# Activations laid out chunk by chunk, first part and rest, tokens of one parity together

## The chip, the cores and the metric

The kernel runs on one core of one Trainium2 chip. The metric is the device time of one execution in microseconds, median over runs; less is better.

## The reference

A two-layer encoder on 256 tokens of 1024 channels, float32. Cut to what matters:

```python
for layer in range(DEPTH):                       # DEPTH = 2
    h = h + token_mixer(rmsnorm(h, norm1), ...)  # sub-layer 1
    h = h + conv_ffn(rmsnorm(h, norm2), ...)     # sub-layer 2
return rmsnorm(h, norm_f)

def token_mixer(xn, ...):
    u, q, k, v, g_pool, g_attn = split(xn @ w_in)     # 1024, 3 x 1536, 2 x 1024 columns
    pooled   = [centred_mean(u of group, window w) - u of group for w in (2, 4, 8, 16)]
    pool_out = (pooled @ w_pool per group) * pool_scale
    attn_out = dilated sliding-window attention, 3 groups of 4 heads of 128, combined
    return (sigmoid(g_pool) * (pool_out @ w_a) + sigmoid(g_attn) * (attn_out @ w_b)) @ w_o

def conv_ffn(xn, ...):
    a, g = split(xn @ w_up)                            # 2816 columns each
    a = depthwise convolution of width 3 along the tokens (a) + conv_b
    return (gelu(a) * g) @ w_down
```

## The kernel before

Every float32 product is made of three products in a reduced float32 format: a number is kept as a first part (a cast) and a rest (the number less the cast), for weights (`wh`, `wl`, lines L177 and L178, by ScalarE and VectorE) and for activations (names ending in `h` and `l`). A product is first x first, first x rest and rest x first, summed in PSUM.

Tokens are dealt by parity: token 2m + t sits in partition m of slot t wherever rows are tokens (`h`, `v`). Where channels are the partitions, an activation was kept as 256 tokens in their order, in tiles of shape `[P, 2, KD, S]` (part, chunk of 128 channels, token).

There are two forms of product.

*Channels out* (`proj`, L485 and L486; `chunk_mm`, L475 to L477). The weight chunk (128x128) is stationary and the activation moves. `proj` makes for each of eight chunks a pair: L485 has `wh` stationary and moves first part and rest together, `x2[:, :, k, :]`, 512 columns that lie in two runs of 256; L486 has `wl` stationary and moves the 256 columns of the first part. Both write one PSUM tile of 512, whose halves are added by `add_up` (L492 on ScalarE, L493 on VectorE) or by lines L951 to L963 for q and k. `proj` is called for u, q, k, the gates, `po @ w_a` and both halves of `w_up`.

*Tokens out* (`v_sum`, L567; `residual_mm`, L497 to L499). 128 tokens of one parity of the activation are stationary, `a[:, k, t::2]`, so every second word; 512 columns of weights move. Used for v, for the four first chunks of the MLP's a (the "entry"), for `w_o` and for `w_down`. For layer 0's v, L640 and L729 do the same from `xuh` and `xul`, which are kept as `[P, KD, 2, P]` (parity, then token of that parity).

The tiles in question: `x2` (the normalised input, written by `to_channels` L454 and L455, in layer 0 by `first_values` L716 and L717), `plh`/`pll` (pooled, L821 and L822), `po2` (pooling's output, L837 and L838), `at2` (attention's output, L920 and L921), `m2` (merged, L1006 and L1007) and `acth`/`actl` (the MLP's activation, L1100 and L1101). Pooling (L802 to L816) and convolution (L1074 to L1078) work along the tokens in order.

The order of work is the program's. A class `Weights` loads weights through SP's queue some pieces ahead and splits them three pieces ahead of use; two pools of four PSUM tiles (`acc`, `mmp`) hold the products. Between stages, after a residual product, the first products of the next stage on one parity are put between the transposes of the other (`fill`).

Of the kernel before, what the change touches and what calls it, by code (L numbers as in the profile page):

```python
# [16 lines left out]
P = 128  # L17
# [187 lines left out]
def encoder(ctx, tc, x, w_in, w_pool, pool_scale, w_a, w_b, w_o, norm1, norm2, w_up, conv_w,  # L205
# [225 lines left out]

    def to_channels(xh, xl, psum, g):

        tag = "acc" if psum is acc else "mm"

        def fin(t, r, xn):
            for n in range(4):
                cc = slice(n * 256, (n + 1) * 256)  # L440
                nc.vector.scalar_tensor_tensor(
                    out=xn[:, cc], in0=h[:, t, cc], scalar=r[:, 0:1], in1=g[:, cc],
                    op0=ALU.mult, op1=ALU.mult,
                )
            for n in range(2):
                pt = psum.tile([P, 4, P], F32, tag=tag, name="xt_ps")
                ks = slice(4 * n, 4 * n + 4)
                for k in range(4):
                    c0 = (4 * n + k) * P
                    nc.tensor.transpose(pt[:, k, :], xn[:, c0 : c0 + P], ident)  # L450
                oh = xh[:, ks, :].rearrange("p k (m t) -> p k t m", t=2)[:, :, t, :]
                ol = xl[:, ks, :].rearrange("p k (m t) -> p k t m", t=2)[:, :, t, :]
                last = [
                    nc.scalar.copy(out=oh, in_=pt),  # L454
                    nc.vector.tensor_sub(out=ol, in0=pt, in1=oh.bitcast(F32)),  # L455
                ]
# [15 lines left out]
    def chunk_mm(ps, wh, wl, xh, xl, nk):  # L472

        for k in range(nk):
            nc.tensor.matmul(ps, wh(k), xh[:, k, :], start=(k == 0), stop=False)  # L475
            nc.tensor.matmul(ps, wh(k), xl[:, k, :], start=False, stop=False)  # L476
            nc.tensor.matmul(ps, wl(k), xh[:, k, :], start=False, stop=(k == nk - 1))  # L477

    def proj(x2, nk=8):


        i, (wh, wl) = W.get()
        ps = mmp.tile([P, 2, S], F32, tag="mm", name="proj_ps")
        for k in range(nk):
            nc.tensor.matmul(ps, wh[:, k, :], x2[:, :, k, :], start=(k == 0), stop=False)  # L485
            nc.tensor.matmul(ps[:, 1], wl[:, k, :], x2[:, 0, k, :], start=False, stop=(k == nk - 1))  # L486
        W.free(i)
        return ps[:, 0], ps[:, 1]

    def add_up(out, sums):  # L490
# [10 lines left out]
    def residual_mm(parts, n, done, hold=4, fill=None):  # L501
# [59 lines left out]

    def v_sum(ps, xh, xl, t, n, piece):

        _, (wh, wl) = piece
        passes = [(xh, wh, 0), (xh, wl, 0), (xl, wh, 0), (xh, wh, 1), (xh, wl, 1), (xl, wh, 1)]
        for m, (a, w, j) in enumerate(passes):
            nc.tensor.matmul(  # L567
                ps, a[:, 2 * n + j, t::2], w[:, j, :], start=(n + m == 0), stop=(n == 3 and m == 5)
            )
# [127 lines left out]
    def first_values(rs, raw_x, fs, done, pe, keep_values):  # L697

        xuh, xul = raw_x
        xh, xl, x2 = channel_tiles()  # L700

# [35 lines left out]
    for l in range(DEPTH):  # L737
# [21 lines left out]
        if l == 0:  # L759
            with tc.manual_schedule():  # L760
                begun = begin_values_of_x()
            x2 = first_values(*begun, keep_values)
            xh, xl = x2[:, 0], x2[:, 1]
        else:
            for g in range(NG):
                held = begun[0] if g == 0 else [W.get() for _ in range(4)]
                for t in range(2):
                    if g + t == 0:
                        ps = begun[1]
                    else:  # L770
                        ps = v_tile()
                        for n in range(4):
                            v_sum(ps, xh, xl, t, n, held[n])
                    keep_values(t, g, ps)
# [9 lines left out]

        plh = big.tile([P, KD, S], F32R, tag="ybig", name="plh")
        pll = big.tile([P, KD, S], F32R, tag="xn", name="pll")
        pooled = {}
        for gi in range(3, -1, -1):
# [30 lines left out]
            )  # L819
            ph, pl = plh[:, 2 * gi : 2 * gi + 2, :], pll[:, 2 * gi : 2 * gi + 2, :]  # L820
# [3 lines left out]
        def pool_out(poh, pol):  # L824
            for j in range(2):
                i, (wh, wl) = W.get()
                for gg in range(2):
                    ph, pl = pooled[2 * j + gg]
                    for oc in range(2):
                        ps = mmp.tile([P, S], F32, tag="mm", name="pool_ps")  # L830
                        cc = slice(oc * P, (oc + 1) * P)
# [4 lines left out]
                        sc = hps[:, l, c : c + 1]  # L836
                        nc.scalar.activation(poh[:, c, :], ps, AF.Copy, scale=sc)  # L837
                        nc.vector.scalar_tensor_tensor(  # L838
                            out=pol[:, c, :], in0=ps, scalar=sc, in1=poh[:, c, :].bitcast(F32),
                            op0=ALU.mult, op1=ALU.subtract,  # L840
# [9 lines left out]
        kk = big.tile([P, NH - HPG, 2, P], F32, tag="k1", name="k")  # L850
        at2 = big.tile([P, 2, HPG, S], F32R, tag="at2", name="at2")
        ath, atl = at2[:, 0], at2[:, 1]
# [51 lines left out]
        def weigh(hh):  # L904
# [6 lines left out]
            for g in (1, 2):  # L911
                hd = (g - 1) * HPG + hh
                for t in range(2):
# [20 lines left out]
        for m, c in enumerate(PAIRS):  # L934
            if m == 1:
                po2 = big.tile([P, 2, KD, S], F32R, tag="m2", name="po2")
                poh, pol = po2[:, 0], po2[:, 1]
                pool_parts = pool_out(poh, pol)
            if m == 2:
# [45 lines left out]
        for c in range(KD):  # L985
# [3 lines left out]
            )  # L989
        m2 = big.tile([P, 2, KD, S], F32R, tag="m2", name="m2")  # L990
        mh, ml = m2[:, 0], m2[:, 1]
        for c4 in range(2):
            ths = [gate(4 * c4 + j) for j in range(4)]
            for j2 in range(2):
                i, (wh, wl) = W.get()
                for j in range(2):
# [8 lines left out]
                    nc.vector.tensor_add(out=m, in0=m, in1=pa[:, c, :])  # L1005
                    nc.scalar.copy(out=mh[:, c, :], in_=m)  # L1006
                    nc.vector.tensor_sub(out=ml[:, c, :], in0=m, in1=mh[:, c, :].bitcast(F32))  # L1007
                W.free(i)

        xh, xl, x2 = channel_tiles()  # L1010
        norm = Norm(to_channels(xh, xl, acc, g2))
        entry = []

        def begin_mlp():
# [3 lines left out]
            for n in range(3):  # L1018
                v_sum(ps, xh, xl, 0, n, held[n])
            entry.extend((held, ps))  # L1020
            return lambda: v_sum(ps, xh, xl, 0, 3, held[3])

        run(residual_mm(lambda k: (mh[:, k, :], ml[:, k, :]), KD, norm.add, fill=begin_mlp))


# [3 lines left out]
            [  # L1029
                big.tile([P, n, S], F32R, tag=f"{tag}{j}", name=f"act{tag}{j}")  # L1030
                for j, n in enumerate((HPG, NH - HPG))
# [23 lines left out]
        for n in range(4):  # L1055
            v_sum(ps, xh, xl, 1, n, held[n])
            if n == 1:
# [7 lines left out]
        def up(f):  # L1065
# [15 lines left out]
            )  # L1081
            g = sm.tile([P, S], F32, tag="p", bufs=3, name="g")
            add_up(g, sums)

# [14 lines left out]
            ah, al = (x[n >= HPG][:, n - HPG * (n >= HPG), :] for x in (acth, actl))  # L1099
# [7 lines left out]
        def begin_values():  # L1107

            ps, held = v_tile(), [W.get() for _ in range(4)]
            for n in range(3):  # L1110
                v_sum(ps, xh, xl, 0, n, held[n])
            begun.extend((held, ps))
            return lambda: v_sum(ps, xh, xl, 0, 3, held[3])

# [10 lines left out]
        if l + 1 < DEPTH:  # L1125
            xh, xl, x2 = channel_tiles()
            late["norm"] = Norm(to_channels(xh, xl, mmp, g1))
        else:
# [32 lines left out]
```

## Time and profile before

| | |
|---|---|
| median of 3 runs | 891.43 us (890.87 to 891.78) |
| profiled execution: own time, span | 890.68 us, 888.9 us |
| TensorE busy, matmuls | 881.2 us (99%), 4913 |
| VectorE busy | 671.2 us (76%) |
| ScalarE busy | 516.0 us (58%) |
| GpSimd busy | 13.7 us (2%) |
| DMA, mean | 185 GB/s, 164.47 MB |
| granted TensorE clock | 0.999 |

How to read it: busy is the time in which an engine had an instruction running. Matmuls are pipelined: the trace gives each a duration that overlaps the next one's, so the sum of durations is more than their time, and the interval from one start to the next tells what one costs. PE is the matmuls, PEld the loads of stationary operands, which overlap them; DVE is VectorE, ACT ScalarE, POOL GpSimd.

### The profile page before, as it was taken

Reading aid. Unit: us, or ns where it says so; the run is one execution under the profiler, and the core shown is the slowest. Engines: PE = TensorE matmul, PEld = TensorE weight load, DVE = VectorE, ACT = ScalarE, POOL = GpSimd, SP = SyncE. Lnnn points to the kernel's source line nnn. Section 1 sums busy time; section 2 is a strip of 40 time slices with the busy share of each in tenths; the row PEclk is TensorE's granted clock in tenths of the full one; section 3 lists DMA queues with packets and bytes.
Section 4 is the critical chain, followed back from the end, with each engine's and each line's share of the span. In section 5 each row is a group of like instructions: output and inputs, shape, how many; then the busy total and the mean of one; then the engine's idle time right before and its main releaser. Section 6 shows DMA issues by size and latency. Waiting matters only on the chain.

```text
span 888.9 us, 12895 instructions
## 1 busy us (share of the span) xinstructions
PE 881.2 (99%) x4913; PEld 764.5 (86%) x4913; DVE 671.2 (76%) x1135; ACT 516.0 (58%) x897; POOL 13.7 (2%) x40
## 2 busy tenths in 40 slices
PE   9999999999999999999999999999999999999997
PEld 7889889889888888888888898888898888888886
DVE  7988786767759978777855977766677698777784
ACT  7746454555647756666545564554555476666662
POOL 2000000000000000000000000000000000000000
PEclk9999999999999999999999999999999999999999
DMA  9669744455545465565636555443557346465531
GB/s 335 227 206 302 235 143 142 144 189 189 188 168 190 153 227 190 168 211 189 237 119 211 168 190 189 144 161 125 190 189 264 106 155 231 166 202 187 180 143 48
DMA packets 125791, 164.47 MB, mean 185 GB/s; under 512 B 2996, under 2 KB 106108, under 8 KB 125601
## 3 DMA queue, kind: packets, MB, share of 16 engines
q1 hardware_dynamic: 125712, 163.65, 55.1%
q8 instruction: 38, 0.62, 0.3%
q14 instruction: 25, 0.20, 0.1%
q10 hardware_dynamic: 16, 0.00, 0.0%
HBM read 162.57 MB, written 3.69 MB: 187 GB/s over the span
## 4 chain that ended last, share of the span: by engine, by line
PE 99%; ACT 0%; POOL 0%; DVE 0%; issue 0%; POOLq 0%; ACTq 0%
PE proj_ps L485 40%; PE proj_ps L486 20%; PE v_ps L567 6%; PE res_ps L497 6%; PE res_ps L499 6%; PE res_ps L498 6%; PE v_ps L729 2%; PE v_ps L640 1%; PE b_ps L477 1%; PE b_ps L475 1%; PE b_ps L476 1%; PE pt_ps L893 1%; PE o_ps L914 1%; PE s_ps L864 1%; PE s_ps L859 1%; PE o_ps L910 1%
## 5 line engine op out<-in xcount | busy, mean ns | idle before, releaser
L485 PE MATMUL proj_ps<-x,wh 128*128 128x512 f32 x1408 | 498.4, 398 | 0.0
L178 DVE TENSOR_TENSOR wl<-raw,wh 128x1024 fp32r<-128x1024 f32 x274 | 334.5, 1224 | 131.0 <-ACT wh L177 129.3
L177 ACT CAST wh<-raw 128x1024 fp32r<-128x1024 f32 x274 | 287.2, 1052 | 201.3 <-PE proj_ps L485 144.6
L486 PE MATMUL proj_ps<-x,wl 128*128 128x256 f32 x1408 | 394.3, 280 | 0.0
L485 PEld LDWEIGHTS proj_ps<-x,wh 128*128 128x128 f32 x1408 | 264.4, 188 | 63.3 <-issue 0.7
L486 PEld LDWEIGHTS proj_ps<-x,wl 128*128 128x128 f32 x1408 | 265.7, 189 | 1.0 <-issue 0.2
L497 PE MATMUL res_ps<-wh,actq 128*128 128x512 f32 (+1 forms) x184 | 70.9, 385 | 0.0
L498 PE MATMUL res_ps<-wl,actq 128*128 128x512 f32 (+1 forms) x184 | 70.7, 384 | 0.0
L499 PE MATMUL res_ps<-wh,actk 128*128 128x512 f32 (+1 forms) x184 | 70.7, 384 | 0.0
L485 PE MATMUL proj_ps<-po,wh 128*128 128x512 f32 x128 | 46.2, 402 | 0.0
L497 PEld LDWEIGHTS res_ps<-wh,actq 128*128 128x128 f32 x184 | 35.7, 194 | 6.8
L499 PEld LDWEIGHTS res_ps<-wh,actk 128*128 128x128 f32 x184 | 35.6, 194 | 6.8
L498 PEld LDWEIGHTS res_ps<-wl,actq 128*128 128x128 f32 x184 | 35.7, 194 | 6.1
L486 PE MATMUL proj_ps<-po,wl 128*128 128x256 f32 x128 | 35.8, 279 | 0.0
L1074 ACT ACTIVATE y<-a,prm 128x256 f32<-128x256 f32 x36 | 21.7, 603 | 19.2 <-DVE a L493 19.1
L1091 ACT ACTIVATE y<-y 128x256 f32<-128x256 f32 x44 | 18.4, 417 | 21.3 <-DVE y L1088 21.3
L485 PEld LDWEIGHTS proj_ps<-po,wh 128*128 128x128 f32 x128 | 24.0, 188 | 5.0
L416 ACT ACTIVATE junk<-h 128x512 f32<-128x512 f32 (+1 forms) x20 | 11.0, 549 | 29.3 <-DVE h L414 29.3
L497 PE MATMUL res_ps<-wh,m 128*128 128x512 f32 (+1 forms) x72 | 26.7, 371 | 0.0
L498 PE MATMUL res_ps<-wl,m 128*128 128x512 f32 (+1 forms) x72 | 26.6, 369 | 0.0
L499 PE MATMUL res_ps<-wh,m 128*128 128x512 f32 (+1 forms) x72 | 26.6, 369 | 0.0
L567 PE MATMUL v_ps<-wh,x 128*128 128x512 f32 x80 | 26.1, 397 | 0.0
(208 smaller groups left out, 1146.1 us busy)
## 6 DMA issues: line engine op xcount, KB each, us to landing
raw<-in_w_in_dram SPq DMA_DIRECT2D x58, 1024.0 KB, 5.6
raw<-in_w_up_dram SPq DMA_DIRECT2D x44, 1024.0 KB, 5.6
raw<-in_w_down_dram SPq DMA_DIRECT2D x22, 1024.0 KB, 4.8
raw<-in_w_a_dram SPq DMA_DIRECT2D x8, 1024.0 KB, 4.8
raw<-in_w_o_dram SPq DMA_DIRECT2D x8, 1024.0 KB, 4.9
raw<-in_w_b_dram SPq DMA_DIRECT2D x4, 1024.0 KB
sk<-fd SPq DMA_DIRECT2D x1, 2560.0 KB
raw<-in_w_pool_dram SPq DMA_DIRECT2D x2, 1024.0 KB
```

What stands on the lines that cost most here:

```text
L177: lambda: nc.scalar.copy(out=h, in_=src),
L178: lambda: nc.vector.tensor_sub(out=l, in0=src, in1=h.bitcast(F32)),
L416: nc.scalar.activation(junk[:, 0 : cc.stop - cc.start], h[:, t, cc], AF.Square, scale=D**-0.5, accum_out=ss[:, n : n + 1],)
L485: nc.tensor.matmul(ps, wh[:, k, :], x2[:, :, k, :], start=(k == 0), stop=False)
L486: nc.tensor.matmul(ps[:, 1], wl[:, k, :], x2[:, 0, k, :], start=False, stop=(k == nk - 1))
L497: nc.tensor.matmul(ps, ah, wh, start=first, stop=False)
L498: nc.tensor.matmul(ps, ah, wl, start=False, stop=False)
L499: nc.tensor.matmul(ps, al, wh, start=False, stop=last)
L567: nc.tensor.matmul(ps, a[:, 2 * n + j, t::2], w[:, j, :], start=(n + m == 0), stop=(n == 3 and m == 5))
L729: nc.tensor.matmul(ps[t], a[:, k, t, :], w[:, j, :], start=(k + m == 0), stop=(k == KD - 1 and m == 2),)
L1074: nc.scalar.activation(y, a, AF.Identity, bias=b, scale=w1)
L1091: nc.scalar.activation(y2, y2, AF.Tanh, scale=c)
```

## The change

All activations that go into products get the layout chunk, part, parity, token: `[P, KD, 2, 2, P]` for `x2` and `po2`, and `[.., 2, P]` in place of `[.., S]` for the others. So the stationary operand of `v_sum` and `residual_mm` is 128 words in a row, and the moving operand of L485, `x2[:, k]`, is one run of 512 words. PSUM results of `proj` then come out with the tokens of one parity together. Where q, k, attention and gates use them, they stay so; where u and a need the tokens in order, `add_up` writes every second word (`in_order`); the MLP's activation goes back in L1095, which reads `y2` every second word and now writes into `g`.

```diff
@@ to_channels
-                oh = xh[:, ks, :].rearrange("p k (m t) -> p k t m", t=2)[:, :, t, :]
-                ol = xl[:, ks, :].rearrange("p k (m t) -> p k t m", t=2)[:, :, t, :]
+                oh, ol = (x2[:, ks, part, t, :] for part in (0, 1))
@@ proj
-            nc.tensor.matmul(ps, wh[:, k, :], x2[:, :, k, :], start=(k == 0), stop=False)
-            nc.tensor.matmul(ps[:, 1], wl[:, k, :], x2[:, 0, k, :], start=False, stop=(k == nk - 1))
+            nc.tensor.matmul(ps, wh[:, k, :], x2[:, k], start=(k == 0), stop=False)
+            nc.tensor.matmul(ps[:, 1], wl[:, k, :], x2[:, k, 0], start=False, stop=(k == nk - 1))
...
+    def halves(a):
+        return a.rearrange("p (t m) -> p t m", t=2)
+
+    def in_order(a):
+        return a.rearrange("p (m t) -> p t m", t=2)
@@ residual_mm
-            row_mm(ps_, ah[:, t::2], al[:, t::2], wh[:, 0, cc], wl[:, 0, cc], start, stop)
+            row_mm(ps_, ah[:, t], al[:, t], wh[:, 0, cc], wl[:, 0, cc], start, stop)
@@ v_sum
-                ps, a[:, 2 * n + j, t::2], w[:, j, :], start=(n + m == 0), stop=(n == 3 and m == 5)
+                ps, x2[:, 2 * n + j, part, t, :], w[:, j, :], start=(n + m == 0),
+                stop=(n == 3 and m == 5),
...
-    def channel_tiles():
-        x2 = big.tile([P, 2, KD, S], F32R, tag="x", name="x2")
-        return x2[:, 0], x2[:, 1], x2
+    def two_parts(tag, name):
+        return big.tile([P, KD, 2, 2, P], F32R, tag=tag, name=name)
@@ first_values
-            oh, ol = (
-                a[:, k : k + 2, :].rearrange("p k (m t) -> p k t m", t=2) for a in (xh, xl)
-            )
+            oh, ol = (x2[:, k : k + 2, part] for part in (0, 1))
@@ pooling
-                add_up(u[:, j, PAD : PAD + S], proj(x2))
+                add_up(in_order(u[:, j, PAD : PAD + S]), [halves(a) for a in proj(x2)])
...
+            pd = pd.rearrange("p k (m t) -> p k t m", t=2)
             nc.scalar.copy(out=ph, in_=pd)
             nc.vector.tensor_sub(out=pl, in0=pd, in1=ph.bitcast(F32))
@@ weigh
-            oh = ath[:, hh, :].rearrange("p (m t) -> p t m", t=2)
-            ol = atl[:, hh, :].rearrange("p (m t) -> p t m", t=2)
+            oh, ol = ath[:, hh], atl[:, hh]
@@ q and k
-                src, rest = (s.rearrange("p (m t) -> p t m", t=2) for s in proj(x2))
+                src, rest = (halves(a) for a in proj(x2))
@@ up (MLP)
-                add_up(a, proj(x2))
+                add_up(in_order(a), [halves(b) for b in proj(x2)])
...
-            g = sm.tile([P, S], F32, tag="p", bufs=3, name="g")
-            add_up(g, sums)
+            g = sm.tile([P, 2, P], F32, tag="p", bufs=3, name="g")
+            add_up(g, [halves(a) for a in sums])
...
-                out=y2, in0=y2, scalar=0.5, in1=g, op0=ALU.mult, op1=ALU.mult
+                out=g, in0=in_order(y2), scalar=0.5, in1=g, op0=ALU.mult, op1=ALU.mult
...
-            nc.scalar.copy(out=ah, in_=y2)
-            nc.vector.tensor_sub(out=al, in0=y2, in1=ah.bitcast(F32))
+            nc.scalar.copy(out=ah, in_=g)
+            nc.vector.tensor_sub(out=al, in0=g, in1=ah.bitcast(F32))
...
```

More of the change, by code (lines that the diff above doesn't have):

```diff
@@ L474, in chunk_mm @@
         for k in range(nk):
-            nc.tensor.matmul(ps, wh(k), xh[:, k, :], start=(k == 0), stop=False)
-            nc.tensor.matmul(ps, wh(k), xl[:, k, :], start=False, stop=False)
-            nc.tensor.matmul(ps, wl(k), xh[:, k, :], start=False, stop=(k == nk - 1))
+            nc.tensor.matmul(ps, wh(k), xh[:, k], start=(k == 0), stop=False)
+            nc.tensor.matmul(ps, wh(k), xl[:, k], start=False, stop=False)
+            nc.tensor.matmul(ps, wl(k), xh[:, k], start=False, stop=(k == nk - 1))
     def proj(x2, nk=8):
@@ L560, in v_tile, with v_sum @@
         return acc.tile([P, 512], F32, tag="acc", name="v_ps")
-    def v_sum(ps, xh, xl, t, n, piece):
+    def v_sum(ps, x2, t, n, piece):
         _, (wh, wl) = piece
-        passes = [(xh, wh, 0), (xh, wl, 0), (xl, wh, 0), (xh, wh, 1), (xh, wl, 1), (xl, wh, 1)]
-        for m, (a, w, j) in enumerate(passes):
+        passes = [(0, wh, 0), (0, wl, 0), (1, wh, 0), (0, wh, 1), (0, wl, 1), (1, wh, 1)]
+        for m, (part, w, j) in enumerate(passes):
             nc.tensor.matmul(
-                ps, a[:, 2 * n + j, t::2], w[:, j, :], start=(n + m == 0), stop=(n == 3 and m == 5)
-            )
-    def channel_tiles():
-        x2 = big.tile([P, 2, KD, S], F32R, tag="x", name="x2")
-        return x2[:, 0], x2[:, 1], x2
+                ps, x2[:, 2 * n + j, part, t, :], w[:, j, :], start=(n + m == 0),
+                stop=(n == 3 and m == 5),
+            )
+    def two_parts(tag, name):
+        return big.tile([P, KD, 2, 2, P], F32R, tag=tag, name=name)
     def begin_values_of_x():
@@ L772, in encoder @@
                         for n in range(4):
-                            v_sum(ps, xh, xl, t, n, held[n])
+                            v_sum(ps, x2, t, n, held[n])
                     keep_values(t, g, ps)
@@ L782, in encoder @@
         g2 = gain(norm2[l])
-        plh = big.tile([P, KD, S], F32R, tag="ybig", name="plh")
-        pll = big.tile([P, KD, S], F32R, tag="xn", name="pll")
+        plh = big.tile([P, KD, 2, P], F32R, tag="ybig", name="plh")
+        pll = big.tile([P, KD, 2, P], F32R, tag="xn", name="pll")
         pooled = {}
@@ L823, in encoder, with pool_out @@
             pooled[gi] = (ph, pl)
-        def pool_out(poh, pol):
+        def pool_out(po2):
             for j in range(2):
@@ L829, in pool_out @@
                     for oc in range(2):
-                        ps = mmp.tile([P, S], F32, tag="mm", name="pool_ps")
+                        ps = mmp.tile([P, 2, P], F32, tag="mm", name="pool_ps")
                         cc = slice(oc * P, (oc + 1) * P)
@@ L850, in encoder @@
         kk = big.tile([P, NH - HPG, 2, P], F32, tag="k1", name="k")
-        at2 = big.tile([P, 2, HPG, S], F32R, tag="at2", name="at2")
+        at2 = big.tile([P, 2, HPG, 2, P], F32R, tag="at2", name="at2")
         ath, atl = at2[:, 0], at2[:, 1]
@@ L935, in encoder @@
             if m == 1:
-                po2 = big.tile([P, 2, KD, S], F32R, tag="m2", name="po2")
-                poh, pol = po2[:, 0], po2[:, 1]
-                pool_parts = pool_out(poh, pol)
+                po2 = two_parts("m2", "po2")
+                pool_parts = pool_out(po2)
             if m == 2:
@@ L989, in encoder @@
             )
-        m2 = big.tile([P, 2, KD, S], F32R, tag="m2", name="m2")
+        m2 = big.tile([P, 2, KD, 2, P], F32R, tag="m2", name="m2")
         mh, ml = m2[:, 0], m2[:, 1]
@@ L1005, in encoder @@
                     nc.vector.tensor_add(out=m, in0=m, in1=pa[:, c, :])
-                    nc.scalar.copy(out=mh[:, c, :], in_=m)
-                    nc.vector.tensor_sub(out=ml[:, c, :], in0=m, in1=mh[:, c, :].bitcast(F32))
+                    m = halves(m)
+                    nc.scalar.copy(out=mh[:, c], in_=m)
+                    nc.vector.tensor_sub(out=ml[:, c], in0=m, in1=mh[:, c].bitcast(F32))
                 W.free(i)
-        xh, xl, x2 = channel_tiles()
-        norm = Norm(to_channels(xh, xl, acc, g2))
+        x2 = two_parts("x", "x2")
+        norm = Norm(to_channels(x2, acc, g2))
         entry = []
@@ L1018, in begin_mlp @@
             for n in range(3):
-                v_sum(ps, xh, xl, 0, n, held[n])
+                v_sum(ps, x2, 0, n, held[n])
             entry.extend((held, ps))
-            return lambda: v_sum(ps, xh, xl, 0, 3, held[3])
-        run(residual_mm(lambda k: (mh[:, k, :], ml[:, k, :]), KD, norm.add, fill=begin_mlp))
+            return lambda: v_sum(ps, x2, 0, 3, held[3])
+        run(residual_mm(lambda k: (mh[:, k], ml[:, k]), KD, norm.add, fill=begin_mlp))
         g1 = gain(norm1[l + 1] if l + 1 < DEPTH else norm_f)
@@ L1029, in encoder @@
             [
-                big.tile([P, n, S], F32R, tag=f"{tag}{j}", name=f"act{tag}{j}")
+                big.tile([P, n, 2, P], F32R, tag=f"{tag}{j}", name=f"act{tag}{j}")
                 for j, n in enumerate((HPG, NH - HPG))
@@ L1055, in encoder @@
         for n in range(4):
-            v_sum(ps, xh, xl, 1, n, held[n])
+            v_sum(ps, x2, 1, n, held[n])
             if n == 1:
@@ L1110, in begin_values @@
             for n in range(3):
-                v_sum(ps, xh, xl, 0, n, held[n])
+                v_sum(ps, x2, 0, n, held[n])
             begun.extend((held, ps))
-            return lambda: v_sum(ps, xh, xl, 0, 3, held[3])
+            return lambda: v_sum(ps, x2, 0, 3, held[3])
         down = residual_mm(
```

17 lines of the change are left out of this document (8 added, 9 removed).

## The prediction

> **What bounds the kernel now.** I read the page first: busy shares, the clock and the chain that ended last; then who TensorE waited for.
>
> ```profile
> PE 881.2 (99%) x4913; PEld 764.5 (86%) x4913; DVE 671.2 (76%) x1135; ACT 516.0 (58%) x897; POOL 13.7 (2%) x40
> PEclk9999999999999999999999999999999999999999
> PE 99%; ACT 0%; POOL 0%; DVE 0%; issue 0%; POOLq 0%; ACTq 0%
> ```
> ```profile
> PE gain_ps L333 <- DVE ones L319: 1.0, 1, 1.0
> PE v_ps L640 <- ACT xuh L596: 0.2, 1, 0.2
> ```
>
> The chain is 99% TensorE at the full clock, and TensorE waits for others 1.2 us in all, both times in the start. So the time is the sum of the matmuls' intervals. A matmul's own duration in the trace (398 ns for 512 columns) overlaps its neighbours' and says nothing here; what counts is the interval from one start to the next. I call it the cadence, and read it from merged pieces of the chain of waits, and from first and last rows of the timeline.
>
> ```profile
> 19.96 21.78 PE v_ps L729 x96
> 452.93 28.00 PE v_ps L567 x120
> ```
> ```profile
> 250.96 0.39 PE L498 MATMUL res_ps<-wl,m 128*128 128x512 f32 x1
> 252.36 0.39 PE L498 MATMUL res_ps<-wl,m 128*128 128x512 f32 x1
> ```
>
> L729 and L567 are the same product: a 128x128 stationary of activations against 512 contiguous columns of weights. L729 reads its stationary operand from `xuh`/`xul`, already laid out with one parity together; L567 takes every second token (`t::2`). L729 runs at 21.78/96 = 226.9 ns, L567 at 28.00/120 = 233.3. The residual products (L497 to L499, also `t::2`) show six intervals between these two rows: 1.40/6 = 233.3 again. So the stride of the stationary operand goes with 6.4 ns a matmul.
>
> The largest part is `proj`: pairs of L485 (512 columns in two runs of 256) and L486 (256 columns).
>
> ```profile
> 178.45:212.00 33.55, 33.41 (x96) 17.99 (x96) 1.00 0.55 184
> 480.99:514.92 33.93, 33.73 (x96) 17.85 (x95) 1.00 0.57 187
> ```
> ```profile
> 178.46 0.47 PE L485 MATMUL proj_ps<-x,wh 128*128 128x512 f32 x1
> 178.78 0.27 PE L486 MATMUL proj_ps<-x,wl 128*128 128x256 f32 x1
> 178.89 0.40 PE L485 MATMUL proj_ps<-x,wh 128*128 128x512 f32 x1
> ...
> 211.83 0.28 PE L475 MATMUL b_ps<-at,wh 128*128 128x256 f32 x1
> ...
> 481.11 0.40 PE L485 MATMUL proj_ps<-x,wh 128*128 128x512 f32 x1
> ...
> 514.68 0.28 PE L475 MATMUL pool_ps<-plh,wh 128*128 128x256 f32 x1
> ```
>
> The first two rows are L485 alone in two windows: 96 pairs each (the page's counts, in the column behind the busy time). From the second pair's start to the next stage are 95 pairs: (211.83 - 178.89)/95 = 346.7 ns in the one stretch, (514.68 - 481.11)/95 = 353.4 in the other. Same instructions, same operand forms, two rhythms; each holds through a whole stretch and changes only where other matmuls come between. How much of either there is: 1442 pairs in the trace are followed by another pair with no restart between (under 365 ns); their mean, from first to last, is 350.9 ns.
>
> ```profile
> 42.12 0.40 PE L485 MATMUL proj_ps<-x,wh 128*128 128x512 f32 x1
> ...
> 42.47 0.40 PE L485 MATMUL proj_ps<-x,wh 128*128 128x512 f32 x1
> ...
> 859.17 0.40 PE L485 MATMUL proj_ps<-x,wh 128*128 128x512 f32 x1
> ...
> 859.52 0.40 PE L485 MATMUL proj_ps<-x,wh 128*128 128x512 f32 x1
> ```
>
> Between 346.7 and 353.4 that is (350.9 - 346.7)/6.7 = 63% in the slower rhythm.
>
> **The change part by part.** No matmul is added or removed and no DMA is touched. Counts:
>
> ```profile
> L485 PE MATMUL proj_ps<-x,wh 128*128 128x512 f32 x1408 | 498.4, 398 | 0.0
> L485 PE MATMUL proj_ps<-po,wh 128*128 128x512 f32 x128 | 46.2, 402 | 0.0
> L497 PE MATMUL res_ps<-wh,actq 128*128 128x512 f32 x168 | 66.3, 395 | 0.0
> L497 PE MATMUL res_ps<-wh,m 128*128 128x512 f32 x56 | 22.1, 394 | 0.0
> ```
>
> *Contiguous stationary, 512 columns.* The residual products are three lines of 168 + 56 each, so 672; `v_sum` (L567) has 240 (six passes for each of 40 calls: four pieces by two parities by five column groups, two of them the MLP's entry). 912 matmuls. The nearest row after the change is L729, which has exactly the new form: 912 x (233.3 - 226.9) = 5.8 us. Bounds: nothing, if the stride is not the cause, and the full 5.8. I take 5.8, since both rows are this kernel's and the form is the same. The remaining 96 residual products have 256 columns:
>
> ```profile
> 880.18 0.28 PE L497 MATMUL res_ps<-wh,actq 128*128 128x256 f32 x1
> 880.90 0.28 PE L497 MATMUL res_ps<-wh,actq 128*128 128x256 f32 x1
> ```
>
> Six intervals, 0.72/6 = 120 ns, with the strided stationary. The contiguous 256-column products go about as fast (b_ps starts at 211.83 and, eight matmuls on, at 212.77: 117.5), so I count nothing for them.
>
> ```profile
> 212.77 0.28 PE L477 MATMUL b_ps<-at,wl 128*128 128x256 f32 x1
> ```
>
> [...]
>
> *One moving run in `proj`.* No row of before has 512 columns in one run alternating with 256. Bounds: per pair, the fast rhythm (346.7) is what two contiguous matmuls cost by themselves as well: 226.9 and 120 make 346.9. The slow rhythm is 6.7 above it. If the split run is what lets a pair fall into the slow rhythm, all 1408 + 128 = 1536 pairs go at 346.7: 1536 x (350.9 - 346.7) = 6.5 us. Better is possible if L485 alone sheds more (178.89 minus 178.78 shows L486 at 0.11 to 0.12; 226.9 + 117 = 344): 1536 x 6.9 = 10.6. Worst of the two known rhythms: all at 353.4, a loss of 1536 x 2.5 = 3.8. I take 6.5, nearest to the sum of the two contiguous rows; besides, the strided stages, after which pairs mostly run slow, are gone.
>
> *Strided evictions move.* The token order has to be restored where pooling and convolution need it: ACT's and DVE's `add_up` for `u` (16) and `a` (36) write every second word, L816's result is read so (8), and L1095 reads `y2` so (44). Contiguous instead become the writes of `x2`, `at2` and the reads for q and k.
>
> ```profile
> L454 ACT CAST x<-xt_ps 128x512 fp32r<-128x512 f32 x12 | 7.4, 617 | 12.1 <-PE xt_ps L450 12.1
> L596 ACT CAST xuh<-xt_ps 128x512 fp32r<-128x512 f32 x3 | 1.8, 589 | 2.4 <-PE xt_ps L593 2.4
> L455 DVE TENSOR_TENSOR x<-xt_ps,x 128x512 fp32r<-128x512 f32 x12 | 8.3, 692 | 9.4 <-ACT x L454 9.4
> L597 DVE TENSOR_TENSOR xul<-xt_ps,xuh 128x512 fp32r<-128x512 f32 x3 | 2.1, 689 | 1.4 <-ACT xuh L596 1.4
> ```
>
> L454/L455 write strided what L596/L597 write contiguous: ACT pays 28 ns for 512 columns, DVE 3. So some 14 ns for each of ACT's 52 copies, and nothing to see on DVE. What hides it is TensorE itself. The tightest place is the MLP's entry:
>
> ```profile
> 272.00:330.00 58.00, 58.00 (x318) 50.15 (x318) 52.58 (x98) 40.96 (x77) 0.00 (x0) 1.00 0.60 197
> ```
>
> The columns behind the width are TensorE, its loads, DVE, ACT: DVE has 58.00 - 52.58 = 5.4 us left there and ACT 17. Were that cover gone, each strided DVE instruction would cost what it grows by; even 50 ns on every one of the window's 98 DVE instructions is 4.9 us, inside the 5.4. TensorE going 1.4% faster takes 0.8 us of it. I count zero.
>
> *New waits.* Interleaving first part and rest in one tile can join waits that were apart (a `v_sum` pass on the first part waiting for DVE's rest too): that is one L455, 0.7 us at most, for each parity at the three normalisations that end in `x2` (L455 x12 is two halves of two parities of three), so 4.2 us in all; queued behind it would be TensorE's next products. TensorE showed no wait at all at these places, though L567 already needs the rest in its third pass; I take 0, and the range holds the 4.2.
>
> **Sum.** 5.8 + 6.5 = 12.3 us. The profiled execution took 890.68 us (span 888.9 and 1.8 around it), so 878.4; the median of the runs is 0.75 above it, which makes 879.1.
>
> **The rivals.**
> - *Two rhythms stay.* The alternation of 512 and 256 columns itself is what can lock in the slow rhythm. For it: pairs also run slow right behind `pool_out`, whose products are all contiguous:
>
> ```profile
> 91.87 0.28 PE L477 MATMUL pool_ps<-plh,wl 128*128 128x256 f32 x1
> 91.99 0.40 PE L485 MATMUL proj_ps<-x,wh 128*128 128x512 f32 x1
> ...
> 111.78 0.28 PE L859 MATMUL s_ps<-kh,qh 128*128 128x256 f32 x1
> 92.10:112.40 20.30, 19.73 (x56) 10.34 (x55) 1.00 0.64 207
> ```
>
> (the last row counts the 56 pairs between: (111.78 - 91.99)/56 = 353.4). Then only the strided term is sure: 891.4 - 5.8 = 885.6, between 882 and 889 as the rhythms fall. That the lowering keeps the moving operand in several runs, so that the change does not do what it says, gives the same.
> - *`proj` sheds more* (344 a pair): 891.4 - 5.8 - 10.6 = 875.0.
> [...]
> - *Slower: a third rhythm.* 256 columns more cost 226.9 - 120 = 106.9 ns, so the 768 columns of a pair take 320.7 and L567 pays 233.3 - 213.8 = 19.5 on top of its 512. If with one run both matmuls of a pair pay that, because the moving stream then meets the next weight load as it does in L567, the pair is 359.7: 1536 x 8.8 = +13.5, less 5.8, is 899.1. It decides from 350.9 + 5.8/1.536 = 354.7 ns a pair. Against it: no undisturbed stretch shows more than 353.4.
>
> **How the numbers follow.** Forecast 879.1, chance 0.50 (its own spread 877 to 881). Two rhythms stay 0.28; more shed 0.08; stride free 0.07; third rhythm 0.07. The range leaves out the third rhythm and the outer part of the others: 875 to 887. A difference of 0.2% (1.8 us) is about what a measurement of this kernel can tell from no change. Faster by more than that: 0.89, which is the forecast, more shed, most of stride free and most of the two rhythms; same 0.04, where the rhythms fall badly or neither term comes; slower 0.07, the third rhythm.
>
> **What would show it.** Right: merged L567 pieces at 226.9 ns a matmul instead of 233.3, residual starts 0.68 apart for three instead of 0.70; `proj` pairs 0.347 apart in every stretch, the MLP's included; TensorE still 99% of the chain and waiting about 1.2 us. The two-rhythms rival: stretches of 353 left. Wrong: pairs above 354.7, or rows of TensorE waiting for ACT or DVE in the MLP's entry as DVE's strided rows (L493, L1095) grow.

## The result, and the profile after

| | before | after |
|---|---|---|
| median (6 runs each) | 891.09 us (890.87 to 891.78) | 886.58 us (886.34 to 887.28) |
| profiled execution: own time, span | 890.68 us, 888.9 us | 886.34 us, 884.6 us |
| granted TensorE clock | 0.999 | 0.998 |

The ratio is 0.9948 [0.9937, 0.9958]: 4.5 us faster, where 12.0 were forecast. The range of 875 to 887 holds it, at its upper end. The case that came is the rival *two rhythms stay* (885.6).

The page after, busy shares and the chain that ended last, and below it whom TensorE waited for (us in total, times, longest):

```profile
PE 876.5 (99%) x4913; PEld 758.8 (86%) x4913; DVE 671.0 (76%) x1135; ACT 515.8 (58%) x897; POOL 13.4 (2%) x40
...
PE 99%; ACT 0%; issue 0%; POOL 0%; DVE 0%; POOLq 0%; ACTq 0%
```
```profile
PE gain_ps L333 <- DVE ones L319: 1.0, 1, 1.0
PE v_ps L649 <- ACT m L185: 0.4, 1, 0.4
PE v_ps L649 <- ACT xuh L605: 0.2, 1, 0.2
```

The bound is where it was: one engine, no wait outside the start (one of 0.4 us there is new). So the 4.3 us between the two profiled executions lie in the cadence of the matmuls. For each matmul I took the interval from its start to the next start and summed by the PSUM tile it writes, over all 4913:

| us | before | after | difference |
|---|---|---|---|
| `proj_ps` | 542.4 | 543.0 | +0.6 |
| `res_ps` | 168.4 | 164.9 | -3.5 |
| `v_ps` | 90.8 | 89.5 | -1.3 |
| all tiles | 881.2 | 876.9 | -4.3 |

The strided stationary operand gave its gain, `proj` gave none. The merged pieces of the chain of waits show the first (start, length, count):

```profile
19.90 21.78 PE v_ps L736 x96
...
451.01 27.23 PE v_ps L574 x120
```

L574 is the `v_sum` that was L567: 27.23/120 = 226.9 ns, the same as L736 (before L729), where it had been 233.3. The timeline of TensorE shows the rest (start, duration, line, tiles):

```profile
127.40 0.40 PE L484 MATMUL proj_ps<-x,wh 128*128 128x512 f32 x1
...
130.17 0.40 PE L484 MATMUL proj_ps<-x,wh 128*128 128x512 f32 x1
...
178.89 0.40 PE L484 MATMUL proj_ps<-x,wh 128*128 128x512 f32 x1
...
211.83 0.28 PE L474 MATMUL b_ps<-at,wh 128*128 128x256 f32 x1
...
248.50 0.39 PE L505 MATMUL res_ps<-wl,m 128*128 128x512 f32 x1
...
250.54 0.39 PE L505 MATMUL res_ps<-wl,m 128*128 128x512 f32 x1
...
320.87 0.40 PE L504 MATMUL res_ps<-wh,actq 128*128 128x512 f32 x1
...
323.20 0.39 PE L505 MATMUL res_ps<-wl,actq 128*128 128x512 f32 x1
...
478.42 0.40 PE L484 MATMUL proj_ps<-x,wh 128*128 128x512 f32 x1
...
511.99 0.28 PE L474 MATMUL pool_ps<-plh,wh 128*128 128x256 f32 x1
...
561.69 0.39 PE L484 MATMUL proj_ps<-x,wh 128*128 128x512 f32 x1
...
564.52 0.40 PE L484 MATMUL proj_ps<-x,wh 128*128 128x512 f32 x1
```

Three readings. *`proj`*: 95 pairs from 178.89 to 211.83 are 346.7 ns each, 95 from 478.42 to 511.99 are 353.4. These are the two rhythms of before, to the tenth of a ns, with the moving operand now in one run. In the fast rhythm every pair is alike (230 and 117 ns from start to start); in the slow one the intervals repeat every three pairs (236, 113, 233, 117, 241, 120). Two other stretches show that no stage owns a rhythm: the calls that begin right behind the scores of layer 0 and of layer 1 consist of the same instructions behind the same instructions (the 438 matmuls ahead of these rows are alike too), and the eight pairs from their second pair on take (130.17 - 127.40)/8 = 346 ns each in the one and (564.52 - 561.69)/8 = 354 in the other. Of the 134 calls that directly follow a call, 89 were slow before (over 2.80 us, 66%) and 98 are slow after (73%). *Residual, steady*: nine intervals from 248.50 to 250.54 are 226.7 ns each. *Residual, behind `proj`*: the first ten intervals, from 320.87 to 323.20, are 233 ns on average. Behind the pairs of `proj` the contiguous cadence takes a while to settle, here and in 14 of the 16 places where residual products follow a `proj`. The same place of before, strided, takes 233 ns as well, which is also its steady cadence, so before could not show this cost:

```profile
321.57 0.40 PE L497 MATMUL res_ps<-wh,actq 128*128 128x512 f32 x1
...
323.90 0.39 PE L498 MATMUL res_ps<-wl,actq 128*128 128x512 f32 x1
```

What moved to ScalarE and VectorE, in the groups of before and then of after (count | busy us, mean ns | idle before):

```profile
L1095 DVE SCALAR_TENSOR_TENSOR y<-y,g 128x256 f32<-128x256 f32 x44 | 18.5, 421 | 0.5
...
L493 DVE TENSOR_TENSOR a<-proj_ps,a 128x256 f32<-128x256 f32 x36 | 15.1, 419 | 0.0
...
L492 ACT COPY a<-proj_ps 128x256 f32<-128x256 f32 x36 | 12.9, 359 | 0.0
```
```profile
L1101 DVE SCALAR_TENSOR_TENSOR g<-y,g 128x256 f32<-128x256 f32 x44 | 18.5, 421 | 0.5
...
L500 DVE TENSOR_TENSOR a<-proj_ps,a 128x256 f32<-128x256 f32 x36 | 15.1, 418 | 0.0
...
L499 ACT COPY a<-proj_ps 128x256 f32<-128x256 f32 x36 | 13.6, 378 | 0.0
```

ScalarE pays 19 ns for a copy whose result is written every second word, VectorE nothing that can be seen. The window of the MLP's entry still has TensorE at all of its 58.00 us and VectorE with 5.7 us left:

```profile
272.00:330.00 58.00, 58.00 (x318) 49.88 (x317) 52.33 (x98) 41.40 (x77) 0.00 (x0) 1.00 0.60 198
```

### The profile page after: what moved, and what is told of

Read it like the earlier page. It is cut to its first block, busy times and chain, and to the rows that moved or that the text cites. A ratio compares the mean times of both kernels' runs of the same rounds, so it can differ in the third digit from the quotient of the medians.

```text
span 884.6 us, 12887 instructions
## 1 busy us (share of the span) xinstructions
PE 876.5 (99%) x4913; PEld 758.8 (86%) x4913; DVE 671.0 (76%) x1135; ACT 515.8 (58%) x897; POOL 13.4 (2%) x40
## 4 chain that ended last, share of the span: by engine, by line
PE 99%; ACT 0%; issue 0%; POOL 0%; DVE 0%; POOLq 0%; ACTq 0%
PE proj_ps L484 41%; PE proj_ps L485 20%; PE res_ps L504 6%; PE res_ps L506 6%; PE v_ps L574 6%; PE res_ps L505 6%; PE v_ps L736 2%; PE v_ps L649 1%; PE b_ps L476 1%; PE b_ps L475 1%; PE b_ps L474 1%; PE pt_ps L900 1%; PE o_ps L921 1%; PE s_ps L871 1%; PE s_ps L866 1%; PE o_ps L917 1%
## 5 line engine op out<-in xcount | busy, mean ns | idle before, releaser
L484 PE MATMUL proj_ps<-x,wh 128*128 128x512 f32 x1408 | 498.9, 398 | 0.0
L485 PE MATMUL proj_ps<-x,wl 128*128 128x256 f32 x1408 | 394.4, 280 | 0.0
L484 PEld LDWEIGHTS proj_ps<-x,wh 128*128 128x128 f32 x1408 | 264.5, 188 | 63.8 <-issue 0.7
L485 PEld LDWEIGHTS proj_ps<-x,wl 128*128 128x128 f32 x1408 | 265.7, 189 | 0.9 <-issue 0.2
L484 PE MATMUL proj_ps<-po,wh 128*128 128x512 f32 x128 | 46.2, 402 | 0.0
L485 PE MATMUL proj_ps<-po,wl 128*128 128x256 f32 x128 | 35.7, 279 | 0.0
L484 PEld LDWEIGHTS proj_ps<-po,wh 128*128 128x128 f32 x128 | 24.0, 188 | 5.1
L987 ACT ACTIVATE gates<-gates 128x256 f32<-128x256 f32 x32 | 13.3, 417 | 21.7 <-DVE gates L500 21.7
```

The source lines that it names most:

```text
L484: nc.tensor.matmul(ps, wh[:, k, :], x2[:, k], start=(k == 0), stop=False)
L485: nc.tensor.matmul(ps[:, 1], wl[:, k, :], x2[:, k, 0], start=False, stop=(k == nk - 1))
L987: nc.scalar.activation(th, th, AF.Tanh, scale=0.5)
```

## The experiments

All ratios are to the kernel before, on the same chip (its medians there 891.04 to 891.08 us). A call is one call of `proj`, eight pairs of matmuls. The diffs are cut (`...`). Line numbers shift by a few from kernel to kernel; tiles name the same products.

### The two halves of the change, each alone

The first has the contiguous stationary operand but keeps the parts outermost, so L485's moving operand stays two runs of 256:

```diff
-        return big.tile([P, KD, 2, 2, P], F32R, tag=tag, name=name)
+        return big.tile([P, 2, KD, 2, P], F32R, tag=tag, name=name)
...
-            nc.tensor.matmul(ps, wh[:, k, :], x2[:, k], start=(k == 0), stop=False)
+            nc.tensor.matmul(ps, wh[:, k, :], x2[:, :, k], start=(k == 0), stop=False)
...
```

> One half of the change alone: stationary operands contiguous as in the changed kernel, but parts kept apart, so that the 512 columns of a proj pair's first matmul still lie in two runs of 256. Theory 1 (the alternation of 512 and 256 columns locks pairs into one of two rhythms, 346.7 or 353.3 ns, by the phase at which a stretch begins; the run split has no part in it): same as the changed kernel, 886.6 us within 1, ratio to before 0.995, v_sum and residual products at 226.7 ns. Rival (the run split does cost, and something else in the change eats its gain): slower or faster than the changed kernel by over 1.5 us, with another share of pairs at 353.3 than its 71%.

Measured: 887.01 us, 0.9948 [0.9934, 0.9962], the whole change's ratio, and as many slow calls, 98 of 134. The chain's piece of `v_sum`:

```profile
451.72 27.23 PE v_ps L574 x120
```

The second is the kernel before with one moving run and the stationary operand still `t::2`:

```diff
-        x2 = big.tile([P, 2, KD, S], F32R, tag="x", name="x2")
-        return x2[:, 0], x2[:, 1], x2
+        x2 = big.tile([P, KD, 2, S], F32R, tag="x", name="x2")
+        return x2[:, :, 0], x2[:, :, 1], x2
...
-            nc.tensor.matmul(ps, wh[:, k, :], x2[:, :, k, :], start=(k == 0), stop=False)
+            nc.tensor.matmul(ps, wh[:, k, :], x2[:, k], start=(k == 0), stop=False)
```

> The other half alone: first part and rest beside each other by chunk, one moving run of 512 in proj, but tokens in order and stationary operands at every second word, as before. Theory 1: no gain, 891 us within 1, v_sum and residual products at 233.3 ns, the two rhythms with about the share of before (65% of the calls at 353.3). Rival (one run helps by itself, and only the new entry from contiguous stages spoils it): up to 6.5 us less, 885, pairs at 346.7.

Measured: 891.02 us, 0.9998 [0.9989, 1.0007].

```profile
453.10 28.00 PE v_ps L567 x120
```

28.00/120 = 233.3 ns; 91 of the 134 calls are slow, where before has 89. What follows: the whole gain comes from the stationary operand, and one moving run is worth nothing that can be measured, alone or with it.

### What a stride of the stationary operand costs

In the kernel after, the four `v_sum` groups of layer 1 read their stationary operand at other strides (24 matmuls each, in the order 2, 4, 3, 8 words); v there is made of other words than the reference's.

```diff
-                ps, x2[:, 2 * n + j, part, t, :], w[:, j, :], start=(n + m == 0),
+                ps, spread(x2, 2 * n + j, part, t, group), w[:, j, :], start=(n + m == 0),
...
+        flat = x2[:, k].rearrange("p a b c -> p (a b c)")
+        if group == 4:
+            return flat[:, 0:256:2]
+        if group == 5:
+            return flat[:, 0:512:4]
+        if group == 6:
+            return flat[:, 0:384:3]
+        if group == 7:
...
+            return x2[:, k : k + 2].rearrange("p k a b c -> p (k a b c)")[:, 0:1024:8]
...
```

> The changed kernel, with the stationary operand of layer 1's last four v_sum calls read at other strides over the same tile, so v there is not the reference's: 24 matmuls of 512 columns each at a stride of 1 word (the call before them), 2, 4, 3 and 8 words, in that order. Theory S1 (cost grows with the memory that a load spans): 226.7, 233.3, then 246.7 for 4, 240 for 3 and more for 8. Rival S2 (a stride costs one step whatever its size): 233.3 for all of 2, 3, 4, 8. [...]

Measured: 887.53 us in one run. The timeline's rows at the groups' borders, and the loads of stationary operands, each in a window inside one group (the last number but one is the mean ns of a load; first the contiguous ones, then 2, 4, 3, 8):

```profile
457.21 0.39 PE L590 MATMUL v_ps<-wh,x 128*128 128x512 f32 x1
...
462.81 0.40 PE L590 MATMUL v_ps<-wh,x 128*128 128x512 f32 x1
...
468.45 0.39 PE L590 MATMUL v_ps<-wh,x 128*128 128x512 f32 x1
...
474.10 0.41 PE L590 MATMUL v_ps<-wh,x 128*128 128x512 f32 x1
...
480.01 0.40 PE L484 MATMUL proj_ps<-x,wh 128*128 128x512 f32 x1
```
```profile
L590 PEld LDWEIGHTS v_ps<-ybig,x 128*128 128x128 f32 x6 | 1.1, 188 | 0.2
...
L590 PEld LDWEIGHTS v_ps<-wh,x 128*128 128x128 f32 x9 | 1.7, 193 | 0.4
...
L590 PEld LDWEIGHTS v_ps<-wh,x 128*128 128x128 f32 x9 | 2.5, 310 | 0.0
...
L590 PEld LDWEIGHTS v_ps<-wh,x 128*128 128x128 f32 x9 | 2.2, 253 | 0.0
...
L590 PEld LDWEIGHTS v_ps<-wh,x 128*128 128x128 f32 x9 | 2.6, 332 | 0.0
```

| stride in words | cadence, ns | load's own duration, ns |
|---|---|---|
| 1 | 226.7 (the steady residual products above) | 188 |
| 2 | 5.60/24 = 233.3 | 193 |
| 3 | 5.65/24 = 235.4 | 253 |
| 4 | 5.64/24 = 235.0 | 310 |
| 8 | 5.91/24 = 246.3 | 332 |

The stride itself is the cause: matmuls of the same shape with the same neighbours, and the cadence is 233.3 at stride 2 and 226.7 without one. Neither expectation holds throughout: the cadence doesn't grow with the stride from 3 to 4 (235.4 and 235.0), and it isn't one step for all (8 takes 246.3). The loads step differently from the cadence. A load's own duration hardly changes at 2 (193 ns against 188) and jumps at 3 and 4 (253 and 310). The cadence pays its 6.6 ns already at 2, where the load takes only 5 ns longer, and only some 2 on top at 3 and 4. At stride 2 a load lies wholly within the matmul before it (in the trace of the kernel before all 240 loads of L567 do); why it costs time all the same is not shown.

### Does the stage set the rhythm?

`proj`'s pairs are shifted by one: h0, h1, l0, h2, l1, ... l7 (h: L484's 512 columns, l: L485's 256), so that a call begins with two matmuls of 512 and ends with two of 256.

```diff
-        for k in range(nk):
+        for kind, k in [("h", 0)] + [p for k in range(1, nk) for p in (("h", k), ("l", k - 1))] + [("l", nk - 1)]:
...
```

> The changed kernel with proj's matmuls in the order 512 (chunk 0), then 512 (chunk k) and 256 (chunk k-1) in turn, then 256 (chunk 7): the alternation stays, but each call begins with two matmuls of 512 columns and ends with two of 256. Theory 1 (what comes just before decides the rhythm): a call that follows another call always meets the same start, so such calls run in one and the same rhythm in every stage, all at 346.7 (then about 881 us) or all at 353.3 (then about 888 us); which of the two it cannot say. Rival (the rhythm belongs to the stage, by what runs beside it): the stages that ran at 346.7 still do and the others still run at 353.3, 886.6 us.

Measured: 886.53 us, 0.995 [0.9936, 0.9963]. The starts of the first and the second of eleven calls that follow each other, and of what comes behind the last, in the stretch which ran fast both before and after:

```profile
182.03 0.39 PE L485 MATMUL proj_ps<-x,wh 128*128 128x512 f32 x1
...
184.82 0.40 PE L485 MATMUL proj_ps<-x,wh 128*128 128x512 f32 x1
...
213.01 0.28 PE L474 MATMUL b_ps<-at,wh 128*128 128x256 f32 x1
```

The first takes 2.79 us, the ten behind it (213.01 - 184.82)/10 = 2.819 each, where eight pairs of 346.7 are 2.774. Over the trace, 129 of the 134 calls that follow a call take 2.815 to 2.822, in every stage; the other five take 2.784 with the fast rhythm's 230 and 117 ns inside, and where a call follows one of them it is slow again. So the rhythm isn't a property of a stage or of its data; the order of the matmuls, within the call and just before it, weighs more. The time alone could not tell this: it is what the rival gave (886.6), and the theory had 888 for calls that are all slow.

### The order within `proj`: groups of eight, two and four

If changing between 512 and 256 columns is what costs, fewer changes are cheaper. First all eight h, then all eight l:

```diff
         for k in range(nk):
             nc.tensor.matmul(ps, wh[:, k, :], x2[:, k], start=(k == 0), stop=False)
+        for k in range(nk):
             nc.tensor.matmul(ps[:, 1], wl[:, k, :], x2[:, k, 0], start=False, stop=(k == nk - 1))
```

> The changed kernel with proj's sixteen matmuls in another order: first the eight of 512 columns, then the eight of 256, same operands and sums. Theory 1: without the alternation each group settles at its own cadence, 226.7 and 120 ns, so eight pairs take 8 x 346.7 in every stretch: 1536 x (351.4 - 346.7) = 7.2 us less than the changed kernel, 879.4, ratio 0.987. Rival (the rhythm is set by what the other engines and DMAs do in that stage): the stages that ran at 353.3 still take 8 x 353.3 a call, 886.6.

Measured: 882.99 us, 0.9904 [0.989, 0.9917]: 3.6 us better than the change, half of what was expected. The rival falls: no call behind a call takes more than 2.795 us, in any stage. The timeline of two calls, the first behind a residual product (512 columns), the second behind a call (256):

```profile
310.08 1.98 PE L484 MATMUL proj_ps<-x,wh 128*128 128x512 f32 x8
311.89 1.12 PE L486 MATMUL proj_ps<-x,wl 128*128 128x256 f32 x8
...
312.85 2.00 PE L484 MATMUL proj_ps<-x,wh 128*128 128x512 f32 x8
314.69 1.11 PE L486 MATMUL proj_ps<-x,wl 128*128 128x256 f32 x8
315.64 0.40 PE L484 MATMUL proj_ps<-x,wh 128*128 128x512 f32 x1
```

The first call's 512-column products take 311.89 - 310.08 = 1.81 us, the second's 314.69 - 312.85 = 1.84. Taken over all such calls of the trace, a call behind 512 columns is 2.766 us (17 calls) and a call behind a call 2.793 (134). The intervals show where: behind 256 columns they begin 233, 236, 228, 233, 231 ns before they settle at 227; behind 512 columns they are 227 from the first. Going the other way, the first 256-column interval is 113 instead of 120. So a change from 256 to 512 costs some 27 ns, spread over five matmuls, and the way back returns 7 or 8. It goes with the columns and not with `proj`: in the kernel after, the residual products behind the 256-column products of `b_ps` begin with the same 233, 236, 228, 233, 231 ns, from 234.64 on.

Halving the changes once more should then pay: two calls' h together, then both calls' l.

```diff
+        for (_, (wh, wl)), ps in zip(held, tiles):
+            for k in range(nk):
+                nc.tensor.matmul(ps, wh[:, k, :], x2[:, k], start=(k == 0), stop=False)
+        for (_, (wh, wl)), ps in zip(held, tiles):
+            for k in range(nk):
+                nc.tensor.matmul(ps[:, 1], wl[:, k, :], x2[:, k, 0], start=False, stop=(k == nk - 1))
...
```

> The grouped order over two calls of proj at a time (where two follow each other): sixteen matmuls of 512 columns, then sixteen of 256, in two PSUM tiles. Theory 2 (a change from 256 to 512 columns costs some 27 ns over the next five matmuls, as the grouped kernel's calls show: 2.793 us after 256 columns, 2.766 after 512): some 92 changes fewer, 92 x 27 = 2.5 us less than the grouped kernel's 883.0, 880.5, ratio 0.988. Rival (holding two PSUM tiles and two weight pieces makes TensorE wait for evictions or splits): no gain or a loss against 883.0, with rows of TensorE waiting for VectorE or ScalarE.

Measured: 884.70 us, 0.9931 [0.9918, 0.9943], so 1.7 us worse than single calls: the rival came. TensorE's waits name the reason:

```profile
PE pool_ps L474 <- DVE k L979: 2.6, 2, 2.1
...
PE pool_ps L474 <- DVE q L979: 0.6, 1, 0.6
```

To pair the calls for q and k, the steps of pooling's product had to go ahead of the pair, and TensorE now stands before them, 3.2 us, for work queued on VectorE. It is a cost of the order of stages and says nothing on the cadence. Where nothing waits, two calls that are paired and follow a call take 5.567 us, against 2 x 2.793 = 5.586 for two single ones: some 20 ns saved for each change left out. That is the 27 less the 7 or 8 of the way back, which goes with it and which the expectation had not taken off.

Groups of two within a call: two h, two l.

```diff
-        for k in range(nk):
+        for kind, k in [(c, k + j) for k in range(0, nk, 2) for c in "hl" for j in range(2)]:
...
```

> The changed kernel with proj's order two of 512 columns, two of 256, and so on. Theory 2 (each change from 256 to 512 costs, and recovery takes five matmuls): the first two after a change cost 233 + 236 instead of 2 x 226.7 and the next two of 256 give back 8, so some 701.5 ns for two pairs and 2.806 us a call against 2.811 in the changed kernel: 885.6 us, ratio 0.994. Rival (only strict alternation by ones locks in the slow rhythm): 2.773 a call, 879.4.

Measured: **880.98 us, 0.9887 [0.9872, 0.9902]**, the best of all, 5.6 us under the change and 10.1 under the kernel before. It lies between the theory's 885.6 and the rival's 879.4, and neither gives it.

```profile
184.45 0.63 PE L485 MATMUL proj_ps<-x,wh 128*128 128x512 f32 x2
184.92 0.40 PE L487 MATMUL proj_ps<-x,wl 128*128 128x256 f32 x2
...
187.24 0.40 PE L485 MATMUL proj_ps<-x,wh 128*128 128x512 f32 x1
```

From 184.45 to 187.24 are eight pairs, 2.79 us. Over all calls it is 2.787, or 348.3 ns a pair (intervals 233, 231, 113, 119 and 233, 236, 116, 112 in turn), in every stretch: the slow rhythm of 353.4 doesn't come up. At a fixed price of 27 - 8 = 19 ns there and back, four changes a call would cost 76 ns and make it slower than the group of eight; it is faster. The price of a change isn't fixed: a group of two pays 10 or 15 ns over 227 where a group of eight pays 26.

The same order in the layout of before (operands split and strided):

```diff
-        for k in range(nk):
-            nc.tensor.matmul(ps, wh[:, k, :], x2[:, :, k, :], start=(k == 0), stop=False)
+        for kind, k in [(c, k + j) for k in range(0, nk, 2) for c in "hl" for j in range(2)]:
...
```

> The kernel before, layout untouched (strided stationary operands, two moving runs), with proj's order two of 512 columns, two of 256, and so on. If the term that the prediction put on the moving run belongs to the order alone: calls that follow a call at 2.787 us as in the changed kernel in that order, where before has 2.809 on average (0.022 x 134 = 2.9 us, and 5 us with the other calls), so some 886, ratio 0.994 to 0.995, v_sum and residual products still at 233.3 ns. Rival (the order helps only with the new layout): 891.

Measured: 886.65 us, 0.9949 [0.9934, 0.9963], as expected. So order and layout are worth some 4.5 us each, and as far as can be measured they add up: 891.04 - 4.4 - 4.5 = 882.1, with 880.98 measured, and the interval of such a time is 1.3 us to either side. Calls here are 2.787 us too, so the moving operand's form makes no difference in this order either, and `res_ps` (168.2) and `v_ps` (91.1) keep their strided times.

Groups of four:

```diff
-        for k in range(nk):
+        for kind, k in [(c, k + j) for k in range(0, nk, 4) for c in "hl" for j in range(4)]:
...
```

> The changed kernel with proj's order four of 512 columns, four of 256, and so on. Theory 2 (a change from 256 to 512 columns costs until five matmuls have passed, a change the other way gives 8 ns back): groups of four lie between groups of two (2.787 us a call after a call) and of eight (2.793), so 2.79 a call and 881 to 882 us, ratio 0.989. Rival (groups of two are a special rhythm): 2.80 or more, slower than 883.

Measured: 885.09 us, 0.993 [0.9914, 0.9947]: 3 to 4 us over the expectation. The rival's condition came (2.80 us a call or more, over 883).

```profile
312.70 1.09 PE L485 MATMUL proj_ps<-x,wh 128*128 128x512 f32 x4
313.63 0.64 PE L487 MATMUL proj_ps<-x,wl 128*128 128x256 f32 x4
...
315.51 0.40 PE L485 MATMUL proj_ps<-x,wh 128*128 128x512 f32 x1
```

315.51 - 312.70 = 2.81 us a call. Side by side, for calls behind a call, against eight times 226.9 + 120, which is 2.775 us; the last two columns sum up the call's own intervals in the trace:

| group | call, us | over 2.775, ns | its 512s over 226.9, ns | its 256s under 120, ns |
|---|---|---|---|---|
| one, fast | 2.773 | -1 | 34 | 36 |
| one, slow | 2.827 | 52 | 76 | 24 |
| two | 2.787 | 12 | 50 | 38 |
| four | 2.807 | 31 | 43 | 12 |
| eight | 2.793 | 18 | 26 | 8 |

The price on the 512s falls with fewer changes, though less than in proportion: 12 ns a change in groups of two, 22 in four, 26 in eight. What the 256s give back isn't the 8 ns a change that the expectations took: groups of two get 38 for four changes, groups of four only 12 for two. That is why two is the best and four the worst of the three. Why the 256s give back so unequally, and what makes groups of one fast or slow, stays open.

## Why the prediction was right or wrong

- **What bounds the kernel: right.** TensorE is 99% of the chain before and after, and every gain or loss but that of the paired calls came mainly out of the intervals between its matmuls.
- **Contiguous stationary operand, 5.8 us: right in the cause, a fifth too large.** `v_sum` went to 226.9 as said, the steady residual products to 226.7. Measured are 3.5 + 1.3 = 4.8 us. The steady cadence was taken for all 912 products; the residual products behind a `proj` first pay the change from 256 columns, and their mean over the trace is 228.1. That the stride is free (0.07 among the chances; only the 6.5 us of `proj` would then come) did not hold: with the stride left in and one moving run, nothing is gained (891.02 us against 891.04), and at stride 2 the cadence goes back to 233.3.
- **One moving run in `proj`, 6.5 us: wrong, this is the step that failed.** Measured +0.6 us, and 0 in the experiment that made only this edit. The step rested on "if the split run is what lets a pair fall into the slow rhythm", and the value was taken because two contiguous cadences add up to 346.9. But two steady cadences don't say what alternating them costs: with one run, too, the same pairs go at 346.7 in one stretch and at 353.4 in another. What weighs in place of the split is the order of 512 and 256 columns: with it alone changed to groups of two, the kernel before gains 4.4 us and no call that follows a call takes over 2.789 us. The rows quoted under the rival two rhythms stay, which had 0.28, couldn't decide it: 56 slow pairs behind `pool_out`, whose operands are all contiguous, speak against the strided stages, but these pairs still had two runs themselves. So the second reason, that the strided stages "after which pairs mostly run slow" are gone, was weak already, and it failed: they are gone and 98 calls of 134 are slow instead of 89. The lower bound, all pairs slow, a loss of 3.8, wasn't reached. What picks the rhythm stays open.
- **Strided evictions, zero: right.** ScalarE's copies grew by 19 ns (14 were estimated), VectorE's by nothing, and the cover at the MLP's entry stood.
- **New waits, zero: right.** TensorE's waits are 1.6 us in all, still in the start; against 1.2 before, one of 0.4 us is new.
- **The sum.** 12.3 forecast, 4.3 in the profiled executions: 1.0 is missing from the first term and 7.1 from the second.
- *A third rhythm* and *`proj` sheds more* did not come: all stretches are at 346.7 or 353.4.

## What to carry to other kernels

When one engine is 99% of the chain, read the intervals between starts, and check any sum of two steady cadences on a row where the two forms alternate: here the alternation could cost more than the two (353.4 ns a pair against 346.9), and the order of the matmuls was worth as much as the whole layout (4.4 and 4.5 us). When two rhythms show with the same instructions, an edit of operands is not a cure until one row shows it; try the order first, it is a change of one line, and try several: groups of two, four and eight gave 880.98, 885.09 and 882.99 us. Keep stationary operands contiguous even where the strided load seems hidden: here the stride of two words cost 6.6 ns a matmul, 4.8 us in all.

## What the runs showed of the hardware

- A stationary operand at every second word cost 6.6 ns per 512-column product (233.3 against 226.7), though its load took 193 ns instead of 188 and lay wholly within the matmul before, in all 240 of L567.
- Alternating 512 and 256 columns ran at 346.7 or at 353.4 ns a pair. In the kernels before and after, a rhythm held until other matmuls came between (for up to twelve calls), and in the kernel after the same call behind the same matmuls went fast in one layer and slow in the other (346 and 354 ns a pair). What tips it there is open.
- Behind a group of eight or more 256-column products, the next five of 512 columns took 233, 236, 228, 233, 231 ns before 227; a group of two 512s paid 10 or 15 ns of this, a group of eight all 26. Behind alternating pairs it was, in the kernel after, ten products at 233 ns on average, in 14 of 16 places.
- Whether 512 moving columns come as one run or as two of 256 made no difference that can be measured: 0.9998 [0.9989, 1.0007].
